# A transformer block on one core: the MLP's two products computed from seven block products each

## The chip, the core and the metric

The kernel runs on one core of a Trainium2 chip. TensorE (PE in the profile) multiplies, VectorE (DVE) and ScalarE (ACT) work element by element, GpSimd (POOL) does a few tiny statistics, and SyncE (SP) issues the transfers between DRAM and the on-chip memory. The metric is the device time of one execution in microseconds.

## The reference, cut to what matters

One decoder block in float32, with 1024 tokens, 1024 features and 4096 hidden features:

```python
x = x + mixed @ w_out                                   # x1
h2 = rms_norm(x, g_mlp)
x = x + jnp.square(jax.nn.relu(h2 @ w_ff1)) @ w_ff2     # the MLP
gate_p = jax.nn.sigmoid(rms_norm(x, g_ple) @ w_ple_gate)
x = x + gate_p * (p @ w_ple)
return rms_norm(x, g_final)
```

`mixed` comes from an attention branch and a retention branch, which the change leaves as they are.

## The kernel before

Every float32 operand is split into a high and a low part in float32r (`split`, L108 on ScalarE for the high part, L109 on VectorE for the low one), and every product is made of three matmuls: high by high, high by low, low by high. A matmul takes a stationary tile of 128 x 128 and 512 moving columns and adds into one of eight PSUM banks; the banks are handed out under the names mm (2), qk (3), sm (2) and po (1).

The x1 stage (L719 to L732) keeps the residual stream `xs` on chip for all eight token tiles, multiplies `mixed` by `w_out` in two halves of 512 columns (`n_steps`, L192 to L194, 24 matmuls for a token tile), adds (L727), norms the rows (`norm_rows`: square L228, statistics L220 and L222, scaling L230) and transposes them (`norm_turn`, L237) into `h2T`.

The MLP then runs over 16 chunks `c` of 256 hidden features. A chunk loads 256 columns of `w_ff1` and 256 rows of `w_ff2` (`load_w`, L121), forms the hidden features transposed (`t_steps`, L178 to L180, 96 matmuls), applies the squared relu (L744, L745) and multiplies by the rows of `w_ff2` (L776, 96 matmuls); each of the 16 resulting banks is added into `xs` (L778). The second chunk also prepares `p` (L762) and `g_final` (L767); the last norms and transposes for the embedding stage (L797 and behind).

The tiles have names with a fixed number of buffers: `S0` to `S11`, `T0` to `T7`, `wh` and `wl` (two each), `raw` (three), `Ga` (two), `Gb`, `s2`, `o`, `sq`. A planner of the kernel language inserts the waits and settles, when the program is built, in which order each engine and each queue issues its instructions; the text gives the priorities. All transfers go through SP's queue.

## Time and profile before

| | us |
|---|---|
| three timed runs, median | 2081.61 |
| lowest and highest | 2080.64, 2084.14 |
| profiled execution, span from first to last instruction | 2082.0 |
| TensorE busy in it | 2049.2 |
| VectorE busy | 1079.0 |
| ScalarE busy | 760.3 |

The profiled execution has no other time than its span, which lies between the lowest and the highest run. The MLP takes the stretch from about 1258 to 1959 us. Matmuls overlap in their pipeline, so the time of one matmul in a list of instructions is longer than the step from one to the next.

### The profile page before, as it was taken

What the parts mean: (1) busy time and instruction counts of PE and PEld (TensorE: products, weight loads), DVE (VectorE), ACT (ScalarE), POOL (GpSimd) and SP (SyncE); (2) the same over time, 40 slices, a digit from 0 to 9 for tenths busy, and PEclk for the clock granted to TensorE, in tenths of its full rate; (3) what the DMA queues carried; (4) which work ended last, traced back from release to release, by engine and by line L of the source; (5) the groups of instructions that cost most, each with busy time, mean ns of one, the idle gap of its engine ahead of it and who ended that gap; (6) DMA issues with size and microseconds to landing.
All of it is one profiled execution on the core that took longest, in us unless ns stands there. A gap on an engine that the chain in (4) does not pass through costs nothing.

```text
span 2082.0 us, 26206 instructions
## 1 busy us (share of the span) xinstructions
PE 2049.2 (98%) x10800; PEld 1748.5 (84%) x10800; DVE 1079.0 (52%) x1853; ACT 760.3 (37%) x1281; POOL 84.7 (4%) x104
## 2 busy tenths in 40 slices
PE   7999999999999999999999999999999999999998
PEld 7999999888887887887888888888888888888786
DVE  5334243566575675766645345544544445444743
ACT  4233233455455554557633132212112221122522
POOL 0000000000000100100000000000000000000100
PEclk9999999999999999999999999999999999999999
DMA  5111111111211211205343410311111111111102
GB/s 181 49 53 41 61 61 51 62 56 51 77 41 52 69 33 61 71 26 172 107 152 100 163 41 21 101 41 41 61 41 60 42 41 61 41 55 46 51 1 81
DMA packets 107848, 136.38 MB, mean 66 GB/s; under 512 B 8656, under 2 KB 79952, under 8 KB 107216
## 3 DMA queue, kind: packets, MB, share of 16 engines
q1 hardware_dynamic: 107728, 134.71, 20.3%
q8 instruction: 84, 1.38, 0.3%
...
## 4 chain that ended last, share of the span: by engine, by line
PE 87%; DVE 7%; ACT 3%; issue 1%; POOL 1%; DMA 1%; SPq 0%; POOLq 0%; DVEq 0%; ACTq 0%
PE qk L776 16%; PE mm L178 14%; PE mm L180 14%; PE mm L179 14%; PE mm L192 7%; PE mm L193 7%; PE mm L194 7%; PE po L565 2%; PE qk L522 2%; DVE S L484 2%; DVE S L524 1%; PE qk L437 1%; PE qk L797 1%; PE sm L549 1%; ACT S L482 1%
## 5 line engine op out<-in xcount | busy, mean ns | idle before, releaser
L178 PE MATMUL mm<-T,wh 128*128 128x512 f32 x1280 | 502.4, 393 | 2.9 <-ACT wh L108 1.4
L180 PE MATMUL mm<-T,wl 128*128 128x512 f32 x1280 | 500.6, 391 | 0.2 <-DVE wl L109 0.2
L179 PE MATMUL mm<-T,wh 128*128 128x512 f32 x1280 | 500.0, 391 | 0.0
L776 PE MATMUL qk<-wh,S 128*128 128x512 f32 x1024 | 319.4, 390 | 0.2 <-DVE S L778 0.2
L108 ACT CAST wh<-raw 128x1024 fp32r<-128x1024 f32 x152 | 156.5, 1049 | 426.7 <-PE qk L776 275.6
L178 PEld LDWEIGHTS mm<-T,wh 128*128 128x128 f32 x1280 | 240.9, 188 | 51.2 <-ACT wh L108 1.8
L180 PEld LDWEIGHTS mm<-T,wl 128*128 128x128 f32 x1280 | 240.6, 188 | 50.4 <-DVE wl L109 0.6
L179 PEld LDWEIGHTS mm<-T,wh 128*128 128x128 f32 x1280 | 240.9, 188 | 46.7
L192 PE MATMUL mm<-wh,T 128*128 128x256 f32 (+1 forms) x896 | 269.4, 301 | 5.3 <-ACT T L108 5.3
L194 PE MATMUL mm<-wh,T 128*128 128x256 f32 (+1 forms) x896 | 268.3, 299 | 0.6 <-DVE T L109 0.6
L193 PE MATMUL mm<-wl,T 128*128 128x256 f32 (+1 forms) x896 | 268.2, 299 | 0.1
L109 DVE TENSOR_TENSOR wl<-raw,wh 128x1024 fp32r<-128x1024 f32 x152 | 182.7, 1221 | 114.6 <-ACT wh L108 71.9
L778 DVE TENSOR_TENSOR S<-qk,S 128x512 f32<-128x512 f32 x256 | 174.5, 689 | 110.9 <-PE qk L776 110.9
L776 PEld LDWEIGHTS qk<-wh,S 128*128 128x128 f32 x1024 | 192.1, 188 | 40.1 <-DVE S L778 0.6
L776 PE MATMUL qk<-wl,S 128*128 128x512 f32 x512 | 199.4, 389 | 0.0
L192 PEld LDWEIGHTS mm<-wh,T 128*128 128x128 f32 x896 | 172.0, 192 | 10.5 <-ACT T L108 5.5
L193 PEld LDWEIGHTS mm<-wl,T 128*128 128x128 f32 x896 | 172.1, 192 | 5.6 <-DVE wl L109 0.7
L194 PEld LDWEIGHTS mm<-wh,T 128*128 128x128 f32 x896 | 171.9, 192 | 5.7 <-DVE T L109 0.9
L529 ACT ACTIVATE S<-S,stat 128x256 f32<-128x256 f32 (+7 forms) x128 | 98.7, 772 | 68.3 <-DVE stat L524 66.9
L745 DVE SCALAR_TENSOR_TENSOR Ga<-mm,Ga 128x512 f32<-128x512 f32 x64 | 44.2, 690 | 145.9 <-ACT Ga L744 145.9
L776 PEld LDWEIGHTS qk<-wl,S 128*128 128x128 f32 x512 | 96.1, 188 | 19.8
L744 ACT ACTIVATE Ga<-mm 128x512 f32<-128x512 f32 x64 | 38.2, 597 | 163.3 <-PE mm L180 163.3
...
## 6 DMA issues: line engine op xcount, KB each, us to landing
raw<-in_w_in SPq DMA_DIRECT2D x64, 512.0 KB, 4.1
raw<-in_w_ff SPq DMA_DIRECT2D x64, 512.0 KB, 3.7
S<-in_x SPq DMA_DIRECT2D x16, 512.0 KB, 6.9
gt_d<-Ga SPq DMA_DIRECT2D x32, 256.0 KB, 2.0
Ga<-gt_d SPq DMA_DIRECT2D x32, 256.0 KB, 2.6
...
ya_d<-o SPq DMA_DIRECT2D x16, 256.0 KB, 2.0
raw<-yr_d SPq DMA_DIRECT2D x8, 512.0 KB, 4.0
```

What stands on the lines that cost most here:

```text
L108: nc.scalar.copy(out=hi, in_=src)
L109: nc.vector.tensor_tensor(out=lo, in0=src, in1=hi.bitcast(F32), op=ALU.subtract)
L178: nc.tensor.matmul(out=ps, lhsT=wh(kt), rhs=ah, start=(kt == 0), stop=False)
L179: nc.tensor.matmul(out=ps, lhsT=wh(kt), rhs=al, start=False, stop=False)
L180: nc.tensor.matmul(out=ps, lhsT=wl(kt), rhs=ah, start=False, stop=(kt == KT - 1))
L192: nc.tensor.matmul(out=ps, lhsT=ah, rhs=wh(kt), start=(kt == 0), stop=False)
L193: nc.tensor.matmul(out=ps, lhsT=ah, rhs=wl(kt), start=False, stop=False)
L194: nc.tensor.matmul(out=ps, lhsT=al, rhs=wh(kt), start=False, stop=(kt == KT - 1))
L529: nc.scalar.activation(out=pc, in_=pc, func=AF.Exp, scale=-1.0, bias=mx[:, 2 * c + n:2 * c + n + 1], accum_out=z[:, c:c + 1])
L745: nc.vector.scalar_tensor_tensor(out=r, in0=ps, scalar=0.0, in1=r, op0=ALU.max, op1=ALU.mult)
L776: nc.tensor.matmul(out=ps, lhsT=l, rhs=r, start=(i == 0), stop=(i == len(mm) - 1))
L778: nc.vector.tensor_tensor(out=xa, in0=ps, in1=xa, op=ALU.add)
```

## The change

Both products of the MLP are cut into blocks of two by two and computed by the scheme of Strassen in Winograd's form: seven block products in place of eight, with sums and differences of blocks before and after.

For the first product the blocks of the normed activations are token half by feature half (`a11`, `a12`, `a22`, and the sums `s1`, `s2o`, `s3`, `s4`); they are formed in the second half of the x1 stage, where x1 itself is spilled to the DRAM tensor `x1_d` half by half. The blocks of `w_ff1` are formed in `ff1_prep` for a unit of 128 + 128 hidden features (`b11`, `b21`, `b22`, `t1` to `t4`). A unit makes the seven products in three banks, of which `pa` takes four in turn, applies the squared relu, forms the seven blocks that the second product needs from its left operand and stores them in the DRAM tensor `u_d`.

The second product runs over three pairs of block products and a single seventh one. A pair holds all eight banks and adds up all 2048 hidden features of its blocks in them, in eight groups of 256; each group loads two blocks of `u_d` and two or three of `w_ff2`. Only after the eighth group are the banks added into the quarters of `xs` (`put_quarters`). The preparation of `p`, the norm and the transposes for the embedding stage are placed beside the groups of the seventh block.

```diff
     SIDE = ("S5", "S8", "S10", "S11")
+    w_out = t["w_out"][0]
+    wq = [load_quad(w_out, quad, 0) for quad in range(2)]
+    for st in range(ST):
+        xa = slot("Ga", F32, (P, HALF), bufs=2)
+        nc.sync.dma_start(out=xa, in_=x_d[st * P:(st + 1) * P, 0:HALF])
+        ps = bank()
+        run(n_steps(mixed, st, lambda kt: wq[kt // 4][0][:, kt % 4, :], lambda kt: wq[kt // 4][1][:, kt % 4, :], ps))
+        nc.vector.tensor_tensor(out=xa, in0=ps, in1=xa, op=ALU.add)
+        nc.sync.dma_start(out=x1_d[:, st, 0:HALF], in_=xa)
...
+    wq = [load_quad(w_out, quad, HALF, SIDE[2 * quad:2 * quad + 2]) for quad in range(2)]
+    gain = slot("s2", F32, (P, 1024))
+    nc.sync.dma_start(out=gain, in_=t["g_mlp"].broadcast_to([P, D]))
+    a11, a12 = op_tiles("S0", "S1"), op_tiles("S2", "S9")
+    f11, f12 = [slot(s).rearrange("p (k s) -> p k s", k=4) for s in ("S3", "S4")]
+    for st in range(ST):
+        row = raw_tile()
+        nc.sync.dma_start(out=row[:, 0:HALF], in_=x1_d[:, st, 0:HALF])
+        nc.sync.dma_start(out=row[:, HALF:D], in_=x_d[st * P:(st + 1) * P, HALF:D])
+        ps = bank()
+        run(n_steps(mixed, st, lambda kt: wq[kt // 4][0][:, kt % 4, :], lambda kt: wq[kt // 4][1][:, kt % 4, :], ps))
+        nc.vector.tensor_tensor(out=row[:, HALF:D], in0=ps, in1=row[:, HALF:D], op=ALU.add)
+        nc.sync.dma_start(out=x1_d[:, st, HALF:D], in_=row[:, HALF:D])
+        xn = slot("Gb", F32, (P, 1024))
+        ss = stat()
...
+        nc.vector.scalar_tensor_tensor(out=xn, in0=row, scalar=r, in1=gain, op0=ALU.mult, op1=ALU.mult)
+        o = (st % 4) * P
...
+        if st < 4:
+            for q, f, (hi, lo) in zip(pt, (f11, f12), (a11, a12)):
+                nc.scalar.copy(out=f[:, :, cs], in_=q)
+                split(q, hi[:, :, cs], lo[:, :, cs])
+            continue
+        if st == 4:
+            a22, s1 = op_tiles("T0", "T1"), op_tiles("T2", "T3")
+            s2o = [slot(s, F32R, bufs=2).rearrange("p (k s) -> p k s", k=4) for s in ("wh", "wl")]
+            s3 = [slot(s, F32R, bufs=2).rearrange("p (k s) -> p k s", k=4) for s in ("wh", "wl")]
+            s4 = op_tiles("S6", "S7")
...
+        f21, f1, f2 = small512("o"), small512("sq"), small512("Ga", 2)
+        nc.scalar.copy(out=f21, in_=pt[0])
+        put(pt[1], a22)
+        nc.vector.tensor_tensor(out=f1, in0=pt[1], in1=f21, op=ALU.add)
+        nc.vector.tensor_tensor(out=f2, in0=f1, in1=f11[:, :, cs], op=ALU.subtract)
+        put(f2, s2o)
+        put(f1, s1)
+        nc.vector.tensor_tensor(out=f11[:, :, cs], in0=f11[:, :, cs], in1=f21, op=ALU.subtract)
+        put(f11[:, :, cs], s3)
+        nc.vector.tensor_tensor(out=f12[:, :, cs], in0=f12[:, :, cs], in1=f2, op=ALU.subtract)
+        put(f12[:, :, cs], s4)
+    UNITS = DFF // 256
+    w1, w2 = t["w_ff1"][0], t["w_ff2"][0]
+    def ff1_prep(u):
+        raw = slot(("T4", "T5")[u % 2])
+        for n in range(2):
+            c0 = n * (DFF // 2) + u * P
+            nc.sync.dma_start(out=raw[:, n * 1024:(n + 1) * 1024].rearrange("p (k n) -> p k n", n=P),
+                              in_=w_block(w1, c0, P, 0, KT))
+        b = raw.rearrange("p (b m) -> p b m", b=4)
+        tt = slot("T6").rearrange("p (b m) -> p b m", b=4)
+        def pair(tag, src):
+            g = slot(tag, F32R).rearrange("p (c m) -> p c m", c=2)
+            split(src, g[:, 0, :], g[:, 1, :])
+            g = g.rearrange("p c (o k n) -> p c o k n", o=2, n=P)
+            return [(g[:, 0, o], g[:, 1, o]) for o in range(2)]
...
+        ops = {}
+        ops["b11"], ops["b21"] = pair("T7", raw[:, 0:1024])
+        yield ops
+        sub(tt[:, 1, :], b[:, 2, :], b[:, 0, :])
+        sub(tt[:, 0, :], b[:, 3, :], tt[:, 1, :])
+        ops["t2"], ops["t1"] = pair("S3", tt[:, 0:2, :].rearrange("p b m -> p (b m)"))
+        yield ops
+        sub(b[:, 2, :], b[:, 3, :], b[:, 2, :])
+        ops["t3"], ops["b22"] = pair("S4", raw[:, 1024:2048])
+        yield ops
+        sub(tt[:, 2, :], b[:, 1, :], tt[:, 0, :])
+        g = slot("raw", F32R, (P, 1024), bufs=3).rearrange("p (c m) -> p c m", c=2)
+        split(tt[:, 2, :], g[:, 0, :], g[:, 1, :])
+        g = g.rearrange("p c (k n) -> p c k n", n=P)
+        ops["t4"] = g[:, 0], g[:, 1]
+        yield ops
+    def product(ps, w, a, first):
+        for k in range(4):
+            for n, (x, y) in enumerate(((w[0], a[0]), (w[0], a[1]), (w[1], a[0]))):
+                nc.tensor.matmul(out=ps, lhsT=x[:, k, :], rhs=y[:, k, :], start=(first and k == 0 and n == 0),
+                                 stop=(k == 3 and n == 2), skip_group_check=True)
+    def relu2(c):
+        nc.vector.scalar_tensor_tensor(out=c, in0=c, scalar=0.0, in1=c, op0=ALU.max, op1=ALU.mult)
+    nxt = ff1_prep(0)
...
+        now = ops
+        nxt = ff1_prep(u + 1) if u + 1 < UNITS else iter(())
+        ux = slot(("S8", "S10")[u % 2]).rearrange("p (i s) -> p i s", i=4)
+        uy = slot(("S11", "S5")[u % 2]).rearrange("p (i s) -> p i s", i=4)
...
+        pa, pb, pc = bank(), bank("qk"), bank("qk")
+        p1 = slot("Ga", F32, (P, HALF), bufs=2)
+        u2 = slot(("o", "sq")[u % 2], F32, (P, HALF))
+        p5 = slot(("s2", "Gb")[u % 2], F32, (P, 1024))[:, 0:HALF]
+        product(pa, now["b11"], a11, True)
+        nc.scalar.copy(out=p1, in_=pa)
+        product(pb, now["b21"], a12, True)
+        add(ux[:, 2, :], pb, p1)
+        relu2(ux[:, 2, :])
+        ops = next(nxt, None)
+        product(pa, now["t2"], s2o, False)
+        nc.scalar.copy(out=u2, in_=pa)
+        product(pc, now["t1"], s1, True)
+        nc.scalar.copy(out=p5, in_=pc)
+        next(nxt, None)
+        product(pa, now["t3"], s3, False)
+        add(ux[:, 3, :], pa, p5)
+        relu2(ux[:, 3, :])
+        add(ux[:, 0, :], ux[:, 2, :], ux[:, 3, :])
+        product(pc, now["b22"], s4, False)
+        add(uy[:, 2, :], pc, u2)
+        relu2(uy[:, 2, :])
+        add(uy[:, 0, :], ux[:, 2, :], uy[:, 2, :])
+        add(uy[:, 2, :], uy[:, 2, :], ux[:, 3, :], ALU.subtract)
+        next(nxt, None)
+        product(pa, now["t4"], a22, False)
+        nc.scalar.activation(out=uy[:, 1, :], in_=pa, func=AF.Relu)
+        nc.scalar.activation(out=uy[:, 1, :], in_=uy[:, 1, :], func=AF.Square)
+        add(ux[:, 1, :], ux[:, 3, :], uy[:, 1, :])
+        nc.sync.dma_start(out=u_d[:, 0:4, u, :], in_=ux)
+        add(uy[:, 1, :], uy[:, 1, :], ux[:, 2, :], ALU.subtract)
+        nc.sync.dma_start(out=u_d[:, 4:7, u, :], in_=uy[:, 0:3, :])
+        next(nxt, None)
     xs = halves(("S3", "S4", "S6", "S7"))
     for st in range(ST):
...
+        nc.sync.dma_start(out=xs(st), in_=x1_d[:, st, :])
+    hilo = iter((("S0", "S1", "S2", "S9"), ("wh", "wl", "wh", "wl"), ("T0", "T1", "T2", "T3")) * 8)
+    raws = iter((("T4", "T5"), ("T6", "T7"), ("S5", "S8"), ("S10", "S11")) * 6)
+    def w2_load(out, block, g):
+        r0 = (block // 2) * (DFF // 2) + g * 256
+        nc.sync.dma_start(out=out.rearrange("p (k n) -> p k n", k=2),
+                          in_=w_block(w2, (block % 2) * HALF, HALF, r0 // P, r0 // P + 2))
+    B11, B12, B21, B22 = range(4)
+    PAIRS = (
+        ((2, 4), (B12, B22), ((0, 0, 1, ALU.subtract),), (((1, 1), (3, 1)), ((0, -1), (1, 1)))),
+        ((0, 1), (B22, B11), ((0, 1, 0, ALU.add),), (((0, 1), (3, 1)), ((2, 1), (3, -1)))),
+        ((3, 6), (B21, B22, B11), ((1, 0, 1, ALU.add), (0, 0, 2, ALU.subtract)),
+         (((0, 1), (2, 1)), ((0, 1),))),
+    )
+    def w2_bank(i):
+        return bank(("mm", "mm", "qk", "qk", "qk", "sm", "sm", "po")[i])
...
+    def put_quarters(ps, goals, i):
+        for q, sign in goals:
+            x = quarter(q, i)
+            nc.vector.tensor_tensor(out=x, in0=x, in1=ps, op=ALU.add if sign > 0 else ALU.subtract)
+    def w2_products(banks, a, b, g):
+        for i, ps in enumerate(banks):
+            m, st = i // 4, i % 4
+            for k in range(2):
+                for n, (x, y) in enumerate(((0, 0), (0, 1), (1, 0))):
+                    nc.tensor.matmul(out=ps, lhsT=a[x][:, m, k, st * P:(st + 1) * P], rhs=b[y][:, m, k, :],
+                                     start=(g == 0 and k == 0 and n == 0), stop=(g == 7 and k == 1 and n == 2))
...
+    for us, blocks, sums, goals in PAIRS:
+        banks = [w2_bank(i) for i in range(8)]
+        for g in range(8):
+            ta, tb = next(raws)
+            ra, rb = slot(ta), slot(tb)
+            rbs = [rb[:, 0:1024], rb[:, 1024:2048]]
+            for j, i in enumerate(us):
+                nc.sync.dma_start(out=ra[:, j * 1024:(j + 1) * 1024].rearrange("p (k s) -> p k s", k=2),
+                                  in_=u_d[:, i, 2 * g:2 * g + 2, :])
+            if len(blocks) == 3:
+                rbs.append(raw_tile())
+            for r, blk in zip(rbs, blocks):
+                w2_load(r, blk, g)
+            for dst, x, y, op in sums:
+                nc.vector.tensor_tensor(out=rbs[dst], in0=rbs[x], in1=rbs[y], op=op)
+            tags = next(hilo)
+            hl = [slot(s, F32R, bufs=2 if s[0] == "w" else 1) for s in tags]
+            split(ra, hl[0], hl[1])
+            split(rb, hl[2], hl[3])
+            w2_products(banks, (v4(hl[0]), v4(hl[1])), (v4(hl[2]), v4(hl[3])), g)
+        for i in range(8):
+            put_quarters(banks[i], goals[i // 4], i % 4)
+    h3T = act_tiles(T_TAGS[0:4], 1)
...
+    banks = [w2_bank(i) for i in (2, 3, 4, 7)]
+    for g in range(8):
+        ra = slot(("s2", "Gb")[g % 2], F32, (P, 1024))
+        rb = slot(("S10", "S11")[g % 2])
+        nc.sync.dma_start(out=ra.rearrange("p (k s) -> p k s", k=2), in_=u_d[:, 5, 2 * g:2 * g + 2, :])
+        for j in range(2):
+            w2_load(rb[:, j * 1024:(j + 1) * 1024], (B11, B12)[j], g)
+        nc.vector.tensor_tensor(out=rb[:, 0:1024], in0=rb[:, 0:1024], in1=rb[:, 1024:2048], op=ALU.add)
+        ha, hb = [slot(s, F32R).rearrange("p (c m) -> p c m", c=2) for s in (("T4", "T5"), ("T6", "T7"))[g % 2]]
+        split(ra, ha[:, 0, :], ha[:, 1, :])
+        split(rb[:, 0:1024], hb[:, 0, :], hb[:, 1, :])
+        w2_products(banks, (v4(ha[:, 0, :]), v4(ha[:, 1, :])), (v4(hb[:, 0, :]), v4(hb[:, 1, :])), g)
+        if g == 0:
+            for st in range(4):
                 norm_rows(xs(st), xn(st))
...
-    for c in range(DFF // 256):
...
+        if g == 1:
...
-        last = c == DFF // 256 - 1
...
-                xa = xs(st)[:, n0:n0 + HALF]
-                nc.vector.tensor_tensor(out=xa, in0=ps, in1=xa, op=ALU.add)
...
+        if 2 <= g < 6:
+            norm_turn(xn, gple, h3T, 0, range(2 * g - 4, 2 * g - 2))
+    for i in range(4):
+        put_quarters(banks[i], ((3, 1),), i)
+    h3T += act_tiles(T_TAGS[4:8], 1)
+    for st in range(4, ST):
+        norm_rows(xs(st), xn(st))
+    gfin = slot("Gb", F32, (P, D))
+    nc.sync.dma_start(out=gfin, in_=t["g_final"].unsqueeze(0).broadcast_to([P, D]))
```

The tensors `x1_d` and `u_d` are new; elsewhere comments and descriptions are gone, and `act_tiles` takes the number of halves as an argument.

## Rows read from the trace of the kernel before

**Rows 1.** The page's span and busy times, with the number of instructions of each engine.

```profile
span 2082.0 us, 26206 instructions
PE 2049.2 (98%) x10800; PEld 1748.5 (84%) x10800; DVE 1079.0 (52%) x1853; ACT 760.3 (37%) x1281; POOL 84.7 (4%) x104
```

**Rows 2.** The page's 40 slices, in tenths of a slice.

```profile
PE   7999999999999999999999999999999999999998
...
DVE  5334243566575675766645345544544445444743
...
PEclk9999999999999999999999999999999999999999
DMA  5111111111211211205343410311111111111102
```

**Rows 3.** Chain in order of time, in the MLP: start, us, engine and line.

```profile
1367.26 21.76 PE qk L776 x96
...
1889.50 21.76 PE qk L776 x96
```

**Rows 4.** Timeline of SP before the x1 stage: start, us, line, transfer.

```profile
1003.16 0.37 SPq L653 DMA_DIRECT2D raw<-ya_d  x1
...
1012.83 0.33 SPq L767 DMA_DIRECT2D Gb<-in_g_final  x1
...
1049.15 0.32 SPq L586 DMA_DIRECT2D ya_d<-o  x1
```

**Rows 5.** Timeline of PE in the MLP's last chunk.

```profile
1949.66 1.04 PE L237 MATMUL sm<-ident,S 128*128 128x128 f32 x8
1950.45 0.47 PE L776 MATMUL qk<-wh,S 128*128 128x512 f32 x1
...
1951.83 0.65 PE L237 MATMUL sm<-ident,S 128*128 128x128 f32 x4
```

**Rows 6.** Groups by line and shape: busy, mean ns, idle before.

```profile
L109 DVE TENSOR_TENSOR wl<-raw,wh 128x1024 fp32r<-128x1024 f32 x152 | 182.7, 1221 | 114.6 <-ACT wh L108 71.9 <-PE sm L549 38.8 <-PE sm L762 3.5
L778 DVE TENSOR_TENSOR S<-qk,S 128x512 f32<-128x512 f32 x256 | 174.5, 689 | 110.9 <-PE qk L776 110.9
...
L108 ACT CAST wh<-raw 128x1024 fp32r<-128x1024 f32 x152 | 156.5, 1049 | 426.7 <-PE qk L776 275.6 <-PE mm L179 106.2 <-PE mm L194 30.8
...
L109 DVE TENSOR_TENSOR S<-Ga,S 128x512 fp32r<-128x512 f32 x64 | 44.2, 690 | 31.6 <-ACT S L108 31.6
...
L744 ACT ACTIVATE Ga<-mm 128x512 f32<-128x512 f32 x64 | 38.2, 597 | 163.3 <-PE mm L180 163.3
...
L268 DVE SCALAR_TENSOR_TENSOR S<-S,stat,Gb 128x1024 f32<-128x1024 f32 x8 | 10.3, 1286 | 4.9 <-POOL stat L222 3.6 <-DMA Gb<-in_g_mix 1.2
```

**Rows 7.** Transfers: count, KB of each, median us from issue to landing.

```profile
raw<-in_w_ff SPq DMA_DIRECT2D x64, 512.0 KB, 3.7
...
gt_d<-Ga SPq DMA_DIRECT2D x32, 256.0 KB, 2.0
```

**Rows 8.** Chain in order of time, in the x1 stage.

```profile
1245.89 1.15 ACT S L228 x2
1247.36 0.56 POOL stat L222
1247.94 0.75 DVE S L230
```

**Rows 9.** Windows of 1 us at the start: busy times, granted clock, DMA share, GB/s.

```profile
13.00:14.00 1.00, 0.00 (x0) 0.00 (x0) 0.00 (x0) 0.37 (x1) 0.00 (x0) 0.50 1.02 415
...
20.00:21.00 1.00, 1.00 (x13) 1.00 (x11) 1.00 (x1) 0.17 (x1) 0.00 (x0) 1.00 0.27 26
```

**Rows 10.** Timeline of PE at the start, with the idle time before.

```profile
15.21 0.58 PE L192 MATMUL mm<-wh,T 128*128 128x256 f32 x1 [5.26 <-ACT T L108]
```

**Rows 11.** Windows of 6 us with transfers in line, columns as in rows 9.

```profile
9.00:15.00 6.00, 0.95 (x8) 0.71 (x7) 1.52 (x2) 2.41 (x3) 0.00 (x0) 0.82 1.03 397
1159.00:1165.00 6.00, 6.00 (x28) 4.75 (x27) 4.69 (x6) 2.52 (x3) 0.00 (x0) 1.00 0.86 267
```

More of the change, by code (lines that the diff above doesn't have):

```diff
@@ L87, in block_kernel @@
     gt_d = dram.tile([P, 16, S], F32, name="gt_d")
+    x1_d = dram.tile([P, ST, D], F32, name="x1_d")
+    u_d = dram.tile([P, 7, DFF // 256, HALF], F32, name="u_d")
     ident = small.tile([P, P], F32, name="ident")
@@ L154, in load_pair, with act_tiles @@
         return f(hi), f(lo)
-    def act_tiles(tags):
+    def act_tiles(tags, n=2):
         out = []
         it = iter(tags)
-        for half in range(2):
+        for half in range(n):
             row = []
@@ new lines, in op_tiles, with small512, put @@
+    def op_tiles(*tags):
+        return [slot(s, F32R).rearrange("p (k s) -> p k s", k=4) for s in tags]
+    wq = [load_quad(w_out, quad, HALF, SIDE[2 * quad:2 * quad + 2]) for quad in range(2)]
[13 more added lines that the diff above has]
+        ss = stat()
+        nc.scalar.activation(out=xn, in_=row, func=AF.Square, accum_out=ss)
+        r = rstd_of(ss, D)
+        nc.vector.scalar_tensor_tensor(out=xn, in0=row, scalar=r, in1=gain, op0=ALU.mult, op1=ALU.mult)
+        o = (st % 4) * P
+        cs = slice(o, o + P)
+        pt = []
+        for quad in range(2):
+            q = bank("sm").rearrange("p (k s) -> p k s", s=P)
+            for k in range(4):
+                kt = quad * 4 + k
+                nc.tensor.transpose(out=q[:, k, :], in_=xn[:, kt * P:(kt + 1) * P], identity=ident)
+            pt.append(q)
+        if st < 4:
[8 more added lines that the diff above has]
+            s4 = op_tiles("S6", "S7")
+        def small512(tag, bufs=1):
+            return slot(tag, F32, (P, HALF), bufs=bufs).rearrange("p (k s) -> p k s", s=P)
+        def put(f, op):
+            split(f, op[0][:, :, cs], op[1][:, :, cs])
+        f21, f1, f2 = small512("o"), small512("sq"), small512("Ga", 2)
[9 more added lines that the diff above has]
+        put(f12[:, :, cs], s4)
@@ new lines, in product @@
+    def product(ps, w, a, first):
+        for k in range(4):
+            for n, (x, y) in enumerate(((w[0], a[0]), (w[0], a[1]), (w[1], a[0]))):
[4 more added lines that the diff above has]
+    nxt = ff1_prep(0)
+    for _ in range(4):
+        ops = next(nxt)
@@ L765, in block_kernel @@
             wph, wpl = load_pair(t["w_ple"][0], 0, ("S0", "S1"))
-            gfin = slot("Gb", F32, (P, D))
-            nc.sync.dma_start(out=gfin, in_=t["g_final"].unsqueeze(0).broadcast_to([P, D]))
-        last = c == DFF // 256 - 1
-        for st in range(ST):
-            ss_ = slice(st * P, (st + 1) * P)
-            for n0 in (0, HALF):
-                ps = bank("qk")
-                mm = [(a[:, k, ss_], w[:, k, n0:n0 + HALF]) for k in range(2)
-                      for a, w in ((uh, w2h), (uh, w2l), (ul, w2h))]
-                for i, (l, r) in enumerate(mm):
-                    nc.tensor.matmul(out=ps, lhsT=l, rhs=r, start=(i == 0), stop=(i == len(mm) - 1))
-                xa = xs(st)[:, n0:n0 + HALF]
-                nc.vector.tensor_tensor(out=xa, in0=ps, in1=xa, op=ALU.add)
-            if last:
-                if st == 0:
-                    xn = halves(SIDE)
-                    h3T = act_tiles(T_TAGS)
-                norm_rows(xs(st), xn(st))
-                if st in (5, 6):
-                    norm_turn(xn, gple, h3T, 0, range((st - 5) * 4, (st - 4) * 4))
+        if 2 <= g < 6:
[7 more added lines that the diff above has]
+    nc.sync.dma_start(out=gfin, in_=t["g_final"].unsqueeze(0).broadcast_to([P, D]))
     ss_a = stat(8)
```

40 lines of the change are left out of this document (13 added, 27 removed).

## Prediction

> **What bounds the kernel now.** I read the page from the top. [rows 1]: TensorE is busy 2049.2 of 2082.0 us, VectorE 1079.0, ScalarE 760.3. [rows 2]: the 40 slices are 52 us each, so the MLP fills slices 25 to 36; there PE stands at 9, the granted clock at 9, DVE at 4 to 5 tenths, DMA at 1 (3 in the first). Matmuls are pipelined, so a busy PE may still hide waits; the chain in order of time settles that. [rows 3] has the first and the last of 13 blocks that repeat: 96 matmuls of the second product take 21.76 us, and from 1367.26 to 1889.50 there are 12 equal periods of 43.52 us. One chunk (256 features, 96 + 96 matmuls) thus costs 43.52 us, or 226.7 ns for each matmul, with no wait in it. The sixteen chunks make 696.3 us. TensorE's stream of matmuls is the bound, and only a change in their number, or a new wait, can move the end.
>
> Second, the order of issue. [rows 4]: the load of `g_final` is written inside the MLP's second chunk, yet it is issued at 1012.83, long before the MLP; a read of `ya_d` goes out at 1003.16, ahead of a store to another part of `ya_d` at 1049.15. [rows 5]: the sixteen transposes of one `norm_turn` call are written as one run, but matmuls of the next token tile stand between them. So engines and the DMA queue do not follow the text: work whose operands are late is passed by, and a spilled tensor is read by region. I therefore price the new code by what each engine has to do in a stretch, not by walking its lines.
>
> **The change, part by part.**
>
> *Matmuls.* The first product goes from 16 x 96 to 16 units x 7 products x 12 = 1344, the second from 16 x 96 to 24 groups x 48 + 8 groups x 24 = 1344. That is 384 fewer; each has the same 128x128 by 128x512 shape as before, so 384 x 226.7 ns = **-87.0 us**. The Trainium skill ("TensorE: Matmul & The Clock Gate", Back-to-back issue gap) gives about 131 ns for a sustained 512-column matmul with its weight load; by that the gain would be 50 us and the forecast 37 us later. The trace does not agree, it shows 226.7 ns, and the row decides.
>
> *Removed vector work.* 256 additions of 689 ns out of PSUM [rows 6] go, 48 come back. They ran under TensorE, so this gives nothing by itself.
>
> *The first product (16 units).* TensorE needs 84 x 226.7 ns = 19.04 us for a unit. VectorE, by [rows 6]: three splits of 1024 (1221 ns), one of 512 (690), four differences and eleven additions or squares of 512 (690 each): 3.66 + 0.69 + 2.76 + 7.59 = 14.7 us, 77% of the unit. ScalarE: three casts of 1049 ns and six smaller operations, each about the relu's 597: 6.7 us. So TensorE stays the longest, but VectorE is fuller than in any slice of [rows 2] (7 tenths). One bank carries four products in turn (b11, t2, t3, t4), read out after each; between two of them stands one product in another bank, 12 x 226.7 ns = 2.72 us. The read-out takes 0.6 to 0.7 us and may find its engine at a 1.05 to 1.22 us split, so about 2 us: covered. If it is late, TensorE waits for that much. Weight tiles have one buffer each, but at least five products (13.6 us) lie between last and next use, for a split of 2.3 us. I take 3 us for the stage, bounds 0 and 16 (1 us for each unit).
>
> *Building the operands (x1 stage).* TensorE's work is unchanged: 2 x 8 x 24 matmuls and 64 transposes. The spill of x1 moves pieces of 256 KB; such a store lands in 2.0 us [rows 7], under a token tile's 24 x 226.7 ns = 5.44 us: nothing, and if that cover were gone, about 2 us at the first tile. New is VectorE's load in token tiles 4 to 7: addition 0.69, scaling by row and gain 1.29 and nine operations of 0.69 [rows 6], so 8.2 us a tile, against TensorE's 5.44 + 0.79 (eight transposes, [rows 5]). Counted from the end of tile 4's product, VectorE needs 4 x 8.2, plus one wait of 2.05 from the start of the square to the start of the scaling (1245.89 to 1247.94 in [rows 8]), plus 4.9 until the third product of unit 0 can start (a 1.22 split, two differences of 0.69, then cast 1.05 and split 1.22 into a tile that tile 7 has just released): 39.7 us. TensorE has meanwhile three tiles and four sets of transposes (19.5), the two products of unit 0 that need only the first half's tokens (5.4), and the same two of unit 1 if they are taken ahead (5.4): 30.4. Idle: 9.3 us, or 14.8 without the last. A gap like that also costs clock: [rows 9, 10] show PE idle for 5.26 us up to 15.21, the granted clock at its lower level (0.50, 1.2 GHz) at 13 and back at 1.00 (2.4 GHz) at 20, so that between four and five us of work ran at half speed: some 2 us lost. The first weights also wait, since their raw buffers hold `mixed` until the last tile's product; this lies inside the same gap. Below: if the last operand's differences are put off (4 x 1.38), 4 us. Above: if every tile repeats the 2.05 us wait and nothing is taken ahead, 45.8 - 24.9 + 2 = 23. I take 14, between 9.3 + 2 and 14.8 + 2.
>
> *From the first product to the second.* The last unit's relu, square, two additions and store take about 0.6 + 0.6 + 1.4 + 2.0 = 4.6 us after the last matmul, but the first two groups read units 0 to 3, their buffers are free during unit 15, and VectorE has 19.04 - 7.59 = 11.4 us there against 2 x 5.8 of preparation. The third group's buffer waits for that store and shares the queue with eight loads of x1: 6.3 MB at the 310 to 397 GB/s of [rows 11] (267 at a DMA share of 0.86 is 310 at full) is 16 to 20 us, with splits done 25 to 29 us after the end where 21.8 are covered. 0 to 7; I take 2, since half of the x1 loads can go before the end.
>
> *The second product.* A group is 48 x 226.7 ns = 10.9 us on TensorE; VectorE needs one sum of 1.22 (two in the third pair) and two splits of 2048, some 2.28 each by extrapolation from 690 and 1221: 5.8 to 7.0; ScalarE 3.8. At a pair's end sixteen additions (11.0 us; twelve in the third) follow the banks as they finish, 1.36 us apart, and a bank is wanted again eight banks later: 0. If that cover fails because they sit behind the next splits, 1.38 + 5.8 = 7.2 at each of three changes, so up to 21.
>
> *The seventh block and the tail.* Eight groups of 5.44 us on TensorE with 1.57 MB each. One buffer's cycle: a 512 KB transfer lands in 3.7 us [rows 7], two more follow at 1.3 to 1.7, then sum, cast, split 3.5: 9.8 to 10.6 us, for two groups' 10.9. Norm pieces of 0.75 ([rows 8]) get in between. 0 to 12; I take 4. The last additions and norms of tiles 4 to 7 are covered by four token tiles of the embedding stage, which need only the first half: 0.
>
> **Sum:** -87.0 + 3 + 14 + 2 + 0 + 4 = -64 us. From the profiled 2082.0 (a span that lies within the three timed runs, median 2081.61, so nothing lies around it) this gives **2018**. With every bound at its low end 1999, at its high end 2074.
>
> **Rivals.** (a) *The gaps are filled:* [rows 5] and the little time in which PE is not busy speak for it (32.8 us in all, [rows 1], 5.26 of them in [rows 10]); then only the operand gap's 4 us stay: about 1999. (b) *VectorE becomes the bound of the first product:* for it, 77% is more than any slice shows, and each unit has chains from bank to VectorE and back; against it, slices with 7 tenths of DVE have PE at 9. At 2 us a unit, 32 in place of 3: 2047. (c) *Slower: transfers bound the second product.* It fetches 128 pieces of 512 KB, 67.1 MB, in 304.7 us, 220 GB/s, where DMA now stands at 1 tenth in most of the MLP [rows 2]. It eats the gain from 67.1 MB / (305 + 64) = 182 GB/s down. If the queue had one transfer in flight at a time, 128 x 3.7 us = 474, 169 more: 2187. Against it, [rows 11]: loads that stand in line on one queue ran at 310 to 397 GB/s, at a full DMA share. (d) *No change*, the point where (c) just decides.
>
> **How the numbers follow.** Forecast 0.62; (a) 0.13; (b) 0.14; (c) and (d) 0.11, of which 0.03 end within 0.2% (4 us, about what a measurement of this kernel can tell from no change) and 0.08 beyond. So faster 0.89, same 0.03, slower 0.08. The forecast's own range is 2005 to 2032. The range goes down to (a) at 1999 and up to 2048, which takes in (b) to 2 us a unit; (c), (d) and the worse part of (b) stay out.
>
> **What would show it.** Right: 10416 matmuls and transposes on PE; in the first product's stretch about 19 us a unit with DVE near 77%; one visible PE gap of 8 to 15 us between the x1 stage and the first unit's third product, with a dip of the granted clock behind it; groups of the second product 10.9 us apart; DMA at 5 to 7 tenths there. Wrong: units of 20 us or more with PE waiting on VectorE or ScalarE (then (b)); PE waiting on DMA or on splits whose loads are late (then (c)); gaps at each change of pair; reads of the spilled sums that wait for its last store.

## The result, and the profile after

The changed kernel takes 2011.41 us (median; 2008.51 to 2012.04), the kernel before, beside it on the same chip, 2082.55: the ratio is 0.9654 (95% interval 0.964 to 0.9668). That is 71 us less; the forecast was 64 less, 2018, with a range of 1999 to 2048.

The page of the changed kernel, for [rows 1]:

```profile
span 2006.7 us, 25935 instructions
...
PE 1967.4 (98%) x10416; PEld 1680.2 (84%) x10416; DVE 1184.6 (59%) x1889; ACT 843.4 (42%) x1321; POOL 84.6 (4%) x104
```

Its 40 slices, now of 50 us each, for [rows 2]:

```profile
PE   8999999999999999999999999899999999999998
...
DVE  6334242576466756856854425876676667767733
...
PEclk9999999999999999999999999999999999999999
DMA  6111111111212112112444243344545986545302
```

There are 384 matmuls fewer, as counted, and TensorE still sets the time. VectorE now stands at 6 to 7 tenths all through the MLP (8 in its first slice), DMA at 3 to 9. One slice, the 26th, has PE at 8: the place between the x1 stage and the first product. The chain in order of time shows the steady part, for [rows 3]:

```profile
1534.66 5.44 PE mm L833 x24
...
1553.70 5.44 PE mm L833 x24
...
1575.46 2.72 PE mm L926 x12
...
1586.34 2.72 PE mm L926 x12
```

The blocks of 24 begin once in each unit of the first product: units are 19.04 us apart, which is 84 x 226.7 ns and nothing more. The second product (L926) follows the last unit without a gap, and its groups are 10.88 us apart. The windows by stage follow: the first product from unit 0's last products on, then the three pairs, then the seventh block. The columns, as in [rows 9], are the stretch and its length, then busy time with the count of instructions of PE, PEld, DVE, ACT and POOL, then the granted clock, the DMA share and GB/s:

```profile
1284.40:1575.30 290.90, 290.90 (x1286) 240.85 (x1284) 210.91 (x289) 105.84 (x137) 0.00 (x0) 1.00 0.51 167
1575.30:1662.40 87.10, 87.10 (x386) 72.08 (x385) 56.32 (x43) 31.24 (x19) 0.00 (x0) 1.00 0.91 338
1662.40:1749.50 87.10, 87.10 (x386) 72.13 (x385) 59.30 (x46) 29.87 (x17) 0.00 (x0) 1.00 0.63 222
1749.50:1836.50 87.00, 87.00 (x386) 72.03 (x385) 60.54 (x49) 30.84 (x22) 0.00 (x0) 1.00 0.48 159
1836.50:1885.50 49.00, 49.00 (x242) 40.94 (x241) 38.44 (x46) 28.94 (x39) 2.76 (x5) 1.00 0.61 212
```

PE is busy for the whole of each. VectorE has 72% of the first product's stretch (13.8 us a unit), and the first pair, which also reads x1 back, moves 338 GB/s at a DMA share of 0.91 with no wait on TensorE. So nearly every loss lies before 1284. TensorE's waits from the x1 stage to the end (us in total, times, longest):

```profile
PE mm L833 <- ACT S L110: 4.3, 1, 4.3
PE sm L759 <- DVE Gb L751: 3.8, 7, 0.6
PE mm L833 <- DVE T L111: 3.2, 2, 2.7
PE mm L833 <- ACT T L110: 1.7, 2, 1.4
```

The four lines sum to 13.0 us. Three of them are the gap at the first product (9.2 us); the second is new in size: the transposes of a token tile wait for its scaling, seven times (before, once, for 0.7 us). The timeline of PE in the gap:

```profile
1256.30 0.73 PE L833 MATMUL mm<-S,T 128*128 128x512 f32 x2 [1.38 <-ACT T L110]
...
1260.19 3.95 PE L833 MATMUL mm<-S,T 128*128 128x512 f32 x10 [2.70 <-DVE T L111]
...
1266.48 1.03 PE L759 MATMUL sm<-ident,Gb 128*128 128x128 f32 x8
...
1269.08 2.59 PE L833 MATMUL mm<-S,T 128*128 128x512 f32 x10 [0.53 <-DVE T L111]
1275.97 0.79 PE L833 MATMUL mm<-wh,S 128*128 128x512 f32 x1 [4.30 <-ACT S L110]
```

Tile 7's matmuls end at about 1254.9. Unit 0's first weights then wait for their cast and their low part (1.38 and 2.70 us), tile 7's transposes stand behind twenty of unit 0's matmuls (1266.48), then the first product of unit 1 is taken ahead (twelve matmuls, the last ten from 1269.08), and unit 0's third product starts at 1275.97, when the cast of t2/t1 into S3 is done. Up to there 36 matmuls of the first product have run: two products of unit 0 and one of unit 1. VectorE in the same stretch:

```profile
1258.92 1.22 DVE L111 TENSOR_TENSOR T<-T,T 128x1024 fp32r<-128x1024 f32 x1
...
1263.67 1.28 DVE L751 SCALAR_TENSOR_TENSOR Gb<-raw,stat,s 128x1024 f32<-128x1024 f32 x1
...
1274.96 0.69 DVE L111 TENSOR_TENSOR S<-S,S 128x512 fp32r<-128x512 f32 x1
```

From 1250 to 1276 VectorE is busy 23.91 of 26 us. The low part of the weights (1258.92) and tile 7's scaling (1263.67) stand in its queue behind tile 6's operand sums. The granted clock, in windows of 2 us:

```profile
1262.00:1264.00 2.00, 2.00 (x7) 1.54 (x6) 2.00 (x4) 1.22 (x2) 0.00 (x0) 0.50 0.00 0
...
1276.00:1278.00 2.00, 2.00 (x4) 1.30 (x5) 2.00 (x3) 1.39 (x2) 0.00 (x0) 0.50 0.00 0
1278.00:1280.00 2.00, 2.00 (x6) 1.58 (x5) 2.00 (x4) 0.00 (x0) 0.00 (x0) 0.50 0.09 20
```

It falls to its lower level (1.2 GHz) twice: just behind the 2.70 us wait (0.76 in the window from 1260), and during the 4.30 us wait (0.67 in the window from 1274).

**The account.** The x1 stage, the first product's end and the second's are cut at the first matmuls of each:

```profile
1156.10 0.39 PE L194 MATMUL mm<-wh,T 128*128 128x512 f32 x1
...
1575.30 2.88 PE L926 MATMUL mm<-S,S 128*128 128x512 f32 x12
...
1885.46 1.52 PE L1012 MATMUL qk<-S,S 128*128 128x512 f32 x6
```

Before, the x1 stage began at 1160.34 and the embedding stage (its first matmul) at 1959.10: 798.76 us. After, 729.36: 69.4 less. Of the two spans' difference of 75.3 us, 4.2 lie ahead of the x1 stage, where nothing changed, and 1.7 in the tail. Those 4.2 are no gain of the change. The first weights' cast was waited for 2.36 us where [rows 10] has 5.26; in the runs below this wait is anything from 2.7 to 4.4. And before, the granted clock was 0.57 from 965 to 969 us, where the changed kernel has 1.00; the same dip stands in nine of the twelve kernels below. Without the 4.2 us the profiled executions differ by 71.1 us, as the medians do. Call *extra* what the x1 stage takes beyond TensorE's own work, that is the second product's start less 16 units, less the x1 stage's start, less 384 x 226.7 ns and 64 transposes ([rows 5]: 0.79 for eight), 93.35 us: 1575.30 - 304.64 - 1156.10 - 93.35 = 21.2 us. The second product and seventh block take 310.16 us, of which 304.7 are matmuls and 4.7 are 48 transposes: 0.7 extra.

### The profile page after: what moved, and what is told of

Read it like the earlier page. It is cut to its first block, busy times and chain, and to the rows that moved or that the text cites. A ratio compares the mean times of both kernels' runs of the same rounds, so it can differ in the third digit from the quotient of the medians.

```text
span 2006.7 us, 25935 instructions
## 1 busy us (share of the span) xinstructions
PE 1967.4 (98%) x10416; PEld 1680.2 (84%) x10416; DVE 1184.6 (59%) x1889; ACT 843.4 (42%) x1321; POOL 84.6 (4%) x104
## 4 chain that ended last, share of the span: by engine, by line
PE 86%; DVE 7%; ACT 3%; issue 1%; DMA 1%; POOL 1%; SPq 0%; POOLq 0%; ACTq 0%; DVEq 0%
PE mm L833 9%; PE mm L180 8%; PE mm L181 8%; PE mm L182 8%; PE mm L196 7%; PE mm L194 7%; PE mm L195 7%; PE qk L926 7%; PE qk L833 7%; PE mm L926 3%; PE sm L926 3%; PE po L567 2%; PE po L926 2%; PE qk L524 2%; DVE S L486 2%
## 5 line engine op out<-in xcount | busy, mean ns | idle before, releaser
L180 PE MATMUL mm<-T,wh 128*128 128x512 f32 x768 | 302.4, 394 | 3.0 <-ACT wh L110 1.5
L182 PE MATMUL mm<-T,wl 128*128 128x512 f32 x768 | 300.9, 392 | 0.1
L181 PE MATMUL mm<-T,wh 128*128 128x512 f32 x768 | 300.1, 391 | 0.0
L180 PEld LDWEIGHTS mm<-T,wh 128*128 128x128 f32 x768 | 144.5, 188 | 31.3 <-ACT wh L110 1.9
L182 PEld LDWEIGHTS mm<-T,wl 128*128 128x128 f32 x768 | 144.2, 188 | 30.3 <-DVE wl L111 0.5
L181 PEld LDWEIGHTS mm<-T,wh 128*128 128x128 f32 x768 | 144.5, 188 | 26.8
L111 DVE TENSOR_TENSOR wl<-raw,wh 128x1024 fp32r<-128x1024 f32 x88 | 105.9, 1221 | 45.1 <-PE sm L551 38.8
L110 ACT CAST wh<-raw 128x1024 fp32r<-128x1024 f32 x88 | 90.9, 1049 | 72.6 <-PE mm L181 55.9
L524 PE MATMUL qk<-S,S 128*128 128x512 f32 (+3 forms) x384 | 92.3, 361 | 3.9 <-DVE stat L526 3.0
L526 DVE CUSTOM_DVE_ANT_0 S<-qk,Gb 128x512 f32<-128x512 f32 (+3 forms) x128 | 72.0, 585 | 35.9 <-PE qk L524 35.6
L833 PE MATMUL mm<-wh,S 128*128 128x512 f32 x256 | 85.9, 397 | 4.3 <-ACT S L110 4.3
L111 DVE TENSOR_TENSOR S<-sm,S 128x512 fp32r<-128x512 f32 (+2 forms) x116 | 63.5, 575 | 35.0 <-ACT S L110 34.5
```

The costliest lines, as they stand in the source:

```text
L110: nc.scalar.copy(out=hi, in_=src)
L111: nc.vector.tensor_tensor(out=lo, in0=src, in1=hi.bitcast(F32), op=ALU.subtract)
L180: nc.tensor.matmul(out=ps, lhsT=wh(kt), rhs=ah, start=(kt == 0), stop=False)
L181: nc.tensor.matmul(out=ps, lhsT=wh(kt), rhs=al, start=False, stop=False)
L182: nc.tensor.matmul(out=ps, lhsT=wl(kt), rhs=ah, start=False, stop=(kt == KT - 1))
L524: nc.tensor.matmul(out=ps, lhsT=qs[:, c, qsl], rhs=kk[:, c, k0:k0 + kw], start=(m == 0), stop=(m == 1))
```

## The experiments

Each is told by its median, beside the changed kernel's 2011.4, and by the *extra* of its profiled execution, worked out in the same way. The before runs beside them had medians of 2081.7 to 2083.4. In the profiled executions the x1 stage starts anywhere from 1156.1 to 1159.0 us, though nothing ahead of it differs: two or three us between medians say little unless the extra agrees. Kernels with the same x1 stage show an extra of 21.2 to 22.1.

**One product at a time.** First product in seven products, second in eight ordinary ones:

```diff
-        add(ux[:, 0, :], ux[:, 2, :], ux[:, 3, :])
...
-        nc.sync.dma_start(out=u_d[:, 0:4, u, :], in_=ux)
+        nc.sync.dma_start(out=u_d[:, 2:4, u, :], in_=ux[:, 2:4, :])
+        nc.sync.dma_start(out=u_d[:, 0:2, u, :], in_=uy[:, 1:3, :])
...
+    H = ((2, 1), (0, 3))
+
+    banks = [w2_bank(i) for i in range(8)]
+    for g in range(16):
+        ta, tb = next(raws)
+        ra, rb = slot(ta), slot(tb)
+        f, gg = g // 8, g % 8
+        nc.sync.dma_start(out=v3(ra[:, 0:1024]), in_=u_d[:, H[0][f], 2 * gg:2 * gg + 2, :])
+        for n in range(2):
+            w2_load(rb[:, n * 1024:(n + 1) * 1024], 2 * f + n, gg)
...
```

> Only the first product is made from seven products; the second is made from the eight ordinary block products (four spilled blocks, a first pass of 16 groups of 48 matmuls and two passes of 16 groups of 24). 192 matmuls of 226.7 ns more than in the changed kernel: 43.5 us. Theory (each matmul that goes is worth 226.7 ns and the seven-fold second product costs nothing besides): 43.5 us slower than the changed kernel, about 2055, 26 to 30 faster than before. Rival (the seven-fold second product hides a loss to its transfers, 0.91 of DMA in its first pair): this kernel moves less in each group, so it is only 30 to 38 us slower than the changed one.

Measured 2055.38 (ratio 0.9871, 0.9855 to 0.9888): 44.0 slower. Divided by 192 matmuls that is 229 ns each, so the seven-fold second product gives its full matmuls back and costs nothing. Extra 22.1, as in the changed kernel.

Second product in seven, first in eight, with a11, a12, a21, a22 split straight from the transposes:

```diff
-            a22, s1 = op_tiles("T0", "T1"), op_tiles("T2", "T3")
-        f21, f1, f2 = small512("o"), small512("sq"), small512("Ga", 2)
...
+            a21, a22 = op_tiles("T0", "T1"), op_tiles("T2", "T3")
+        for q, (hi, lo) in zip(pt, (a11, a12) if st < 4 else (a21, a22)):
+            split(q, hi[:, :, cs], lo[:, :, cs])
```

> Only the second product is made from seven products; the first is made from eight ordinary ones with four operands, and no sums of activations are built in the x1 stage. Theory (the operand sums cost about 21 us in the x1 stage, the rest is free): 43.5 us of matmuls come back and about 21 us go, so 18 to 26 slower than the changed kernel, about 2030 to 2037. Rival (the 21 us are the price of going from one stage to the next and of norm and transposes, whatever operands are built): 38 to 44 slower, about 2051.

Measured 2051.24 (0.9853, 0.9838 to 0.9868): 39.8 slower, the rival's number. But its waits of PE hold a line that the changed kernel has not:

```profile
PE mm L874 <- ACT wh L110: 5.6, 1, 5.6
```

That is the second product's second group, whose raw tile T6 held the last unit's weights in this kernel; its second product takes 319.0 us where the changed kernel's takes 310.2. So this kernel had a fault of its own, and that it met the rival's number is chance. The same with the two tiles exchanged:

```diff
-        ops["b12"], ops["b22"] = pair(("S4", "T6")[u % 2], raw[:, 1024:2048])
+        ops["b12"], ops["b22"] = pair(("T6", "S4")[u % 2], raw[:, 1024:2048])
```

> As the run with only the second product in seven, with two weight tiles exchanged: there the second product's third load waited for a tile that the last unit's weights held until its end (5.6 us of waiting, about 12 us in all), a cost of that kernel's own. Theory (by the traces the operand sums cost 21.2 - 9.2 = 12 us of the x1 stage's extra 21; the other 9 come from normalizing and transposing token tile by token tile): 43.5 - 12 = 29 to 34 us slower than the changed kernel, about 2042. Rival (the operand sums cost 4 us or less): again 38 to 44 slower.

Measured 2042.79 (0.9807, 0.9794 to 0.9821): 31.4 slower; the fault had cost 8.5 us, not the 12 supposed. Extra: 1609.77 - 348.2 - 1158.88 - 93.35 = 9.3. So 12 of the 21 us go with the operand sums and all that hangs on them, the wait for S3 below among it. Nine stay without them: 4.5 are waits of the transposes for the scaling (eight times), 1.6 waits for the first weights, and 3.2 were not told apart. In the window 1250 to 1276 VectorE is busy 13.27 us here, TensorE 23.38 at full clock:

```profile
1250.00:1276.00 26.00, 23.38 (x109) 18.40 (x108) 13.27 (x17) 9.43 (x14) 1.10 (x2) 1.00 0.95 283
```

**VectorE's work in the gap.**

```diff
         def put(f, op):
-            split(f, op[0][:, :, cs], op[1][:, :, cs])
+            nc.scalar.copy(out=op[0][:, :, cs], in_=f)
...
+    a22, s1, s2o, s3, s4 = [(o[0], o[0]) for o in (a22, s1, s2o, s3, s4)]
```

> Left out: the low parts of the five operands that are built from token tiles 4 to 7; their high parts stand in for them in the matmuls. Twenty operations of 0.69 us, 13.8 us of VectorE, go from the stretch before the first product; TensorE's and ScalarE's work stays. Theory (VectorE's backlog sets the gap, the late transposes and the clock dips behind them): VectorE falls to 4.8 us a token tile, under TensorE's 6.2, and 12 to 19 us of the extra 21 go: about 1992 to 1999. Rival (the chain from the last tile's square to the operands is latency, with loads and hand-overs between engines): at most 4 us go.

Measured 2004.23 (0.9627, 0.9612 to 0.9641): 7.2 faster; extra 15.7. Neither number came: taking 13.8 us from VectorE returns 5.5 in this stage. With the low parts gone the transposes still wait 4.0 us and the casts and low parts of the first units' weights hold PE for 6.2:

```profile
PE sm L759 <- DVE Gb L751: 4.0, 7, 0.6
PE mm L834 <- ACT T L110: 3.5, 2, 1.7
PE mm L834 <- ACT S L110: 1.8, 1, 1.8
PE mm L834 <- DVE T L111: 0.9, 1, 0.9
```

So VectorE's backlog is one part of the gap; that the chain of hand-overs behind the last tile is the other is a reading of these waits, which no run tests by itself.

```diff
-        nc.vector.tensor_tensor(out=f2, in0=f1, in1=f11[:, :, cs], op=ALU.subtract)
+        nc.gpsimd.tensor_tensor(out=f2, in0=f1, in1=f11[:, :, cs], op=ALU.subtract)
```

and the same for `f11 - f21` and `f12 - f2`:

> Three of the nine operations per token tile 4 to 7 (f2, f11 - f21, f12 - f2, all SBUF to SBUF) go from VectorE to GpSimd, nothing left out. VectorE falls from 8.2 to 6.1 us a tile, about TensorE's 6.2. By GpSimd's own row (a scalar operation of 512 takes 774 ns) three take 2.3 to 4 us a tile. Theory (VectorE's throughput): 5 to 12 us faster than the changed kernel. Rival (latency of the chain): no gain, or up to 3 us slower, since each hand-over between engines is added.

Measured 2015.41 (0.9682, 0.9667 to 0.9696): 4.0 slower; extra 24.7. VectorE's groups in the stretch first (0.69 us each in the changed kernel), then the timelines of GpSimd and of VectorE:

```profile
L111 DVE TENSOR_TENSOR wl<-Ga,wh 128x512 fp32r<-128x512 f32 x4 | 6.5, 1614 | 0.4
L111 DVE TENSOR_TENSOR T<-sq,T 128x512 fp32r<-128x512 f32 x4 | 6.1, 1514 | 0.2
```

```profile
1252.53 1.29 POOL L782 TENSOR_TENSOR Ga<-sq,S 128x512 f32<-128x512 f32 x1 [4.66 <-DVE sq L781]
1253.90 1.62 POOL L785 TENSOR_TENSOR S<-S,o 128x512 f32<-128x512 f32 x1
```

```profile
1253.14 1.23 DVE L111 TENSOR_TENSOR T<-sq,T 128x512 fp32r<-128x512 f32 x1
1254.51 1.56 DVE L111 TENSOR_TENSOR wl<-Ga,wh 128x512 fp32r<-128x512 f32 x1
...
1257.75 1.28 DVE L751 SCALAR_TENSOR_TENSOR Gb<-raw,stat,s 128x1024 f32<-128x1024 f32 x1 [1.61 <-POOL stat L224]
```

Two of GpSimd's operations end at 1253.82 and 1255.52; the two of VectorE that began beneath them take 1.23 and 1.56 us and end 0.55 us after each. Most of what GpSimd took over, VectorE spent beneath it. The Trainium skill ("SBUF — State Buffer", SBUF: two separate sides) says that a GpSimd operation and a VectorE operation with two inputs in SBUF lock a shared pair of ports for a whole instruction, and the later one blocks; these rows agree. A second cost shows in the last row: the norm's statistics (L224) are GpSimd's too and now stand behind its differences, so VectorE's scaling waits 1.61 us for them (0.44 in the changed kernel), and TensorE's transposes for the scaling 9.3 us in all, where it was 3.8:

```profile
PE sm L759 <- DVE Gb L751: 9.3, 8, 2.8
```

So the run does not show what a lighter VectorE would give, for little was taken from it.

**The last tile's buffer.** Unit 0's pairs get tiles that nobody holds:

```diff
-        ops["t2"], ops["t1"] = pair("S3", tt[:, 0:2, :].rearrange("p b m -> p (b m)"))
+        ops["t2"], ops["t1"] = pair("S3" if u else "S10", tt[:, 0:2, :].rearrange("p b m -> p (b m)"))
...
-        ops["t3"], ops["b22"] = pair("S4", raw[:, 1024:2048])
+        ops["t3"], ops["b22"] = pair("S4" if u else "S5", raw[:, 1024:2048])
```

> Only unit 0's weight pairs t2/t1 and t3/b22 are put into tiles S10 and S5 (free until unit 1's sums), not into S3 and S4, which hold f11 and f12 until token tile 7's last readers. Theory (the 4.30 us wait for the cast of S3 is the release of f11 by VectorE's last operations): the third product starts when t2, t1 and s2o are there, some 2.5 us earlier: 2 to 4 us faster than the changed kernel, second clock dip shorter. Rival (VectorE's queue, whatever tile): the cast comes no earlier, 0 to 1 us.

Measured 2004.48 (0.9631, 0.9617 to 0.9644): 6.9 faster by the medians; extra 15.1. In place of the wait of 4.30 us stands this one, and the second clock dip is gone:

```profile
1275.24 0.73 PE L833 MATMUL qk<-T,S 128*128 128x512 f32 x2 [0.72 <-ACT S L110]
```

```profile
1276.00:1278.00 2.00, 2.00 (x10) 1.62 (x10) 2.00 (x5) 1.35 (x3) 0.00 (x0) 1.00 0.00 0
```

The wait was mostly the release of f11, as the theory had it: counted from the x1 stage's start, the cast comes 3.6 us earlier, and with the dip the stage gains 6.1. Not all of it reaches the end. The second product takes 311.9 us here, 310.2 in the changed kernel (its third group waits 0.8 us for its operands' cast and low part), so that from the x1 stage on the two profiled executions differ by 4.4 us. The other 2.5 of the 6.9 are not shown to be the edit's. The intervals of this kernel's ratio and of the changed kernel's overlap slightly, but the extra of the stage and two more runs with the same edit (0.9627 and 0.9628, below) say the same.

Three attempts on the rest, all on top of it. Order of VectorE's operations:

```diff
+        if later:
+            later.pop()()
...
+        if st < ST - 1:
+            put(pt[1], a22)
+
+        def rest(f21=f21, f1=f1, put=put, cs=cs):
...
+        later.append(rest)
+    later.pop()()
+    put(pt[1], a22)
```

> As the run with own tiles for unit 0's weights, and the SBUF part of a token tile's operands stands behind the scaling of the next tile, a22 of the last tile at the end. Same operations, none left out. Theory (late are tile 7's scaling, 3.6 us behind tile 6's operands in VectorE's queue, its transposes behind twenty matmuls, and what follows): third product 5 to 8 us earlier, so 5 to 9 us faster than the changed kernel, about 2003 to 2006. Rival (VectorE's total in the stretch decides, since it stood idle for only 3.5 us between 1250 and 1276): at most 3.5 us, about that of the own tiles alone.

Measured 2010.50 (0.9655, 0.9642 to 0.9669), extra 20.0: it gave back nearly all that the own tiles had won. Tile 7's transposes now came ahead of unit 0's matmuls and waited 3.46 us for the scaling, and the low part of the unit's weights 2.11 us more behind them.

```diff
-        for k in range(4):
-            for n, (x, y) in enumerate(((w[0], a[0]), (w[0], a[1]), (w[1], a[0]))):
+        late = ((w[0], a[1]), (w[1], a[0]))
+        for n, (x, y) in enumerate(((w[0], a[0]),) + (late if a is a11 or a is a12 else late[::-1])):
+            for k in range(4):
```

> As the run with own tiles for unit 0's weights, and in each of the first product's seven products the four matmuls of high part by high part stand ahead of the eight with a low part (same matmuls, other order). Theory (TensorE's 2.7 us wait at the first weights' low part, and the clock dip behind it, cost what PE could have done meanwhile): eight more matmuls, 1.8 us, are ready with the high parts alone, and PE's gap shrinks to about 1 us: 2 to 5 us faster than with own tiles alone. Rival (VectorE's queue sets the third product's start anyway, so PE only waits later): 0 to 1 us.

Measured 2005.87 (0.9627, 0.9613 to 0.964), extra 16.1: the rival. The wait of 2.7 us and its dip are gone, but PE then waits 1.29, 0.74 and 2.08 us further on, and the clock dips in the last of these (0.50 from 1272 to 1276, shown at the end).

```diff
+        for c in (slice(0, HALF), slice(HALF, D)):
+            nc.vector.scalar_tensor_tensor(out=xn[:, c], in0=row[:, c], scalar=r, in1=gain[:, c],
+                                           op0=ALU.mult, op1=ALU.mult)
```

> As the run with the high parts first, and the scaling by row and gain of a token tile is made in two halves of 512 (1.37 in place of 1.28 us), so that four transposes can start after the first. Theory (eight waits of 0.55 us for the scaling, 3.8 us, are the second part of the x1 stage's loss): 2 to 4 us faster than with the high parts first alone. Rival (the order on TensorE follows the moment at which the scaling is expected, so the transposes move up as well and wait as long): 0, or some 1 us slower.

Measured 2008.72 (0.9642, 0.9629 to 0.9655), extra 18.4: the rival again, though 2.9 us slower than the high parts first, where it had said one at most. The transposes waited eight times, 4.8 us in all.

**The transposes.**

```diff
+        if st in (1, 2, 3, 4):
+            first_half(st - 1, turned(xn))
         xn = slot("Gb", F32, (P, 1024))
```

(`turned` holds the eight transposes, `first_half` the copies and splits; both stand behind the next tile's matmuls.)

> As the run with own tiles for unit 0's weights, and the transposes and splits of token tiles 0 to 3 stand behind the next tile's matmuls (same operations). Theory (each set of transposes that TensorE reaches before its scaling is done costs the wait of 0.55 us and some 0.3 us around it; that, with tile by tile norms, is most of the 9 us of the x1 stage that operand sums do not explain): four of seven waits go, 2 to 3.5 us faster than with own tiles alone. Rival (tiles 4 to 7 find VectorE with the work that was put off, four times 1.4 us, and the gap behind them grows by as much): 0 to 2 us slower.

Measured 2006.61 (0.9628, 0.9614 to 0.9641), extra 16.5. Both halves of the expectation came true: the waits at tiles 0 to 3 are gone (2.2 us left of 3.8), and the gap behind tile 7 became one:

```profile
PE mm L842 <- DVE T L111: 7.1, 1, 7.1
PE sm L745 <- DVE Gb L769: 2.2, 3, 1.0
```

```profile
1250.00:1276.00 26.00, 16.16 (x63) 11.93 (x63) 24.32 (x37) 15.54 (x26) 2.32 (x2) 0.74 0.43 117
```

What TensorE no longer waited for in the tiles, it waited for at the end of them, at VectorE, and the clock was 0.74 over these 26 us (0.93 with own tiles alone).

**The rivals (b) and (c).**

```diff
+        for _ in range(6):
+            nc.vector.tensor_tensor(out=p1, in0=p1, in1=u2, op=ALU.add)
```

> Six additions of 512 more on VectorE in each unit of the first product (on a copy that is read no more): 6 x 0.685 = 4.1 us, from 13.8 to about 17.9 of 19.04 us. Theory (TensorE bounds the unit, VectorE's free quarter is truly free): 0 to 16 us slower than the changed kernel, at most 1 us a unit. Rival b (VectorE bounds the unit already through its chains): 30 to 66 us slower.

Measured 2011.58 (0.9663, 0.965 to 0.9676): no change. From 1300 to 1577 VectorE is busy 253.19 of 277 us, TensorE 276.19 (it waits for VectorE once, 0.8 us):

```profile
1300.00:1577.00 277.00, 276.19 (x1219) 228.38 (x1218) 253.19 (x360) 98.17 (x129) 0.00 (x0) 1.00 0.51 170
```

```diff
+            for i in us:
+                nc.sync.dma_start(out=raw_tile().rearrange("p (k s) -> p k s", k=2), in_=u_d[:, i, 2 * g:2 * g + 2, :])
```

> The second product's first three passes read each spilled sum a second time, into a tile that nothing uses: 48 transfers of 512 KB more, 25.2 MB, from 2.1 to 3.1 MB for a group of 10.88 us, 289 GB/s. Theory (transfers are covered with a third to spare where no x1 loads share the queue): 0 to 8 us slower than the changed kernel, nearly all in the first pair, which stood at a DMA share of 0.91 and must now move 29 + 8.4 MB at some 370 GB/s: up to 15 us if that doesn't go. Rival c (transfers bound the second product from about 220 GB/s up): groups of 14 us and more in all three pairs, 60 to 90 us slower.

Measured 2017.45 (0.969, 0.9677 to 0.9703): 6.0 slower. The three pairs:

```profile
1576.70:1663.70 87.00, 82.59 (x358) 67.64 (x357) 48.45 (x32) 31.40 (x18) 0.00 (x0) 0.98 1.03 394
1663.70:1750.70 87.00, 87.00 (x385) 72.06 (x384) 59.10 (x42) 32.11 (x17) 0.00 (x0) 1.00 0.81 309
1750.70:1837.70 87.00, 87.00 (x385) 72.04 (x384) 64.34 (x53) 28.34 (x18) 0.00 (x0) 1.00 0.79 292
```

Only the first pair, full at 394 GB/s, holds TensorE up (4.4 us, and the clock is 0.98 there, which makes up to 1.7 more); the others, with half as many bytes again, leave it at 87.00 of 87.00.

## Why the prediction was right, and where its terms were off

- **Matmuls, -87.0:** right. First product alone in seven: 229 ns for each matmul that the other left in. The 131 ns that the Trainium skill gives ("TensorE: Matmul & The Clock Gate", Back-to-back issue gap) would have made the gain of 192 matmuls, as an estimate, 25 us; 44 were measured.
- **First product, +3 (0 to 16):** 0. Units are 19.04 us to the hundredth, with VectorE at 72% where 77% was forecast. Rival (b) is out with a margin: even at 91% the unit stays TensorE's.
- **Operand gap, +14 (4 to 23):** this is the term that was mis-sized; it measured 21.2. Its 9.3 us of idle time look met, since the three waits at the first product sum to 9.2, but that is chance. They rest on both products of unit 1 being taken ahead, and only one was (36 matmuls before 1275.97, not 48; why, no run shows). With one the prediction's own working gives 39.7 - 27.7 = 12.0. In its terms the stretch from the end of tile 4's product (1233.7) to the third product took 42.3 us, where 39.7 were reckoned, against 27.7 of TensorE's work: 14.6 lost. Some 2.8 more went at half clock behind it, and the rest, 3.8, in the tiles before, which the prediction had at nothing. The clock was put at 2 us for one dip; there were two, and by windows of 2 us, busy time times what the clock lacked, they took 0.43 + 1.0 + 0.22 (1260 to 1266) and 1.0 + 1.0 + 0.76 (1276 to 1282), 4.4 us. And the transposes were counted as TensorE's work alone: they wait 3.8 us. By cause, then, the 21.2 are 9.2 of waits at the first product, 3.8 of waits for the scaling, 4.4 of clock, and 3.8 that were not told apart. By the run with four ordinary operands, 9 of the 21 stay without any sums, and the prediction had nothing for these.
- **What sets the gap:** the step "VectorE needs 39.7 us, TensorE has 30.4" named the engine rightly, but not the place: the 4.30 us wait was mostly the release of S3 from f11, a buffer which this step only passed by ("a tile that tile 7 has just released"). Own tiles for it were worth 6 us of the stage and 4.4 by the end. For the rest, three orders of the same work moved the wait and none made the stage shorter; that VectorE's total in the stretch decides is what late_turn supports, while no_low shows that it isn't alone. Which hand-over holds what is left stays open.
- **First to second product, +2, and the seventh block with the tail, +4:** 0 and 0.7 with no gap at the changes of pairs. With own tiles, where the first product ends sooner, the third group does wait (0.8 us), the place that the first of these terms had named. Rival (a), all gaps filled, is what happened everywhere but at the operand gap.
- **Rival (c):** transfers. Loads stand in line at up to 394 GB/s, and the second product needs about 220. Half as many bytes again cost 6 us; what would eat the gain was not tried.
- **The sum:** 23 us of costs were forecast. The stages from x1 to the end of the second product show 798.76 - 729.36 = 69.4 less, so 17.6 of costs: 21.9 after, less 4.3 that the same stages lost before (798.76 less 3456 matmuls and 112 transposes, 794.4). With the tail's 1.7 that makes the 71.1: 87.0 - 17.6 + 1.7. The operand term was too low, the others too high, and the 4.3 that went with the old stages had no term; that the sum came within 7 us owes something to these errors of both signs.

The kernel with own tiles for unit 0's weights, at 2004.5 us, is the fastest that ran with all of the work, though high_first and late_turn don't differ from it measurably.
